# Output buffers, split distance and build steps of a decoder block's last projection tiles

## The chip, the cores and the metric

The kernel runs on one core of a Trainium2 chip. A core has a matrix engine (TensorE, PE in the profile; PEld is its weight load), a vector engine (VectorE, DVE), an activation engine (ScalarE, ACT), GpSimd (POOL) and SyncE (SP), which here only starts transfers between the chip's main memory (DRAM) and the on-chip memory (SBUF). Matrix products land in accumulators (PSUM). Every engine works through its own list of instructions in the order in which they stand, and waits at an instruction until what that instruction needs has happened; instructions on different engines are tied by semaphores alone. The metric is the device time of one run in microseconds (us); lower is better.

## The reference

One decoder layer on a sequence of 2048 positions and 1024 channels, in float32. A normalised input `h` is projected to eight blocks of 1024 columns; one half feeds a recurrent branch, the other an attention branch; each branch is multiplied by its gate and projected back, the two are merged with gates computed from `h`, and one more projection with a residual and a last normalisation gives the output:

```
y_rnn  = (hr * silu(z_rnn)) @ w_out_rnn
y_attn = (o * silu(z_attn)) @ w_out_attn
merged = sigmoid(g_r + bg_r) * y_rnn + sigmoid(g_a + bg_a) * y_attn
x      = x + gate * (merged @ w_o)
out    = rms_norm(x, g_final)
```

The changed code computes the third line's sum for part of `y_attn`, tile by tile, and at the same time prepares `w_o` for the fourth.

## The kernel before, in words

**Products in three parts.** float32 products are made from operands that are split into a high part (`hi_act`, line 158, on ACT) and a low rest (`lo_pool`, line 164, on POOL, or `lo_dve`, line 167, on DVE). `mm3` multiplies high by high, high by low and low by high: three matmuls of 128x512 per 128 rows of the inner dimension, all recorded at line 150.

**The projection generator.** `steps` works through 64 tiles of 128 output rows by 512 positions: eight jobs of eight tiles, the first four for `w_out_rnn`, the last four for `w_out_attn`. A tile is eight steps (`k` from 0 to 7), and a step is one `mm3`, so a tile has 24 matmuls. Weights come in half tiles numbered `x = 2 * t + k // 4`. The first 40 tiles (`TAIL0`) are spread between the units of the attention as filler. The last 24, tiles 40 to 63, run behind it without other matmuls, 192 steps in all, step `s` being `k` of tile `40 + s // 8`. Jobs change at steps 0, 64 and 128. This stretch is called the tail here.

**What one tail tile needs.** Two half tiles of weights of 256 KB are loaded on SP (line 1675) into a ring of six buffers (`S0` to `S3`, `st3`, `st4`), five half tiles ahead, and split by `split_w`: the high part on ACT, the low part on DVE for even half tiles and on POOL for odd ones. Two gate tiles of 256 KB (`gaT`, the sigmoid gate, and `mrT`, the recurrent branch's share) are loaded on SP by `load_g` (line 1715). When the tile's matmuls are done, `evict` multiplies the accumulator by the gate (line 1720) and adds the share (line 1722) on DVE, in place in the gate's buffer; `store` (line 1727) sends that buffer to `meT` on SP. There are two accumulators `pj`. `evict` of tile `t - 1` stands at `k == 1` of tile `t`, its `store` at `k == 4`, the gate load of tile `t + 1` at `k == 3`. Gates have four buffers named `fg`; every third tile takes `s1` and `s2` in their place.

**Operands of the next job.** The eight right operands of a job (`yh`, `yl`) are loaded and split at steps that stand in `LATE_LOAD_Y` and `LATE_SPLIT_Y`, where step 8 is the first step of the new job. Operands 5 and 6 land in `st1`, 7 in `st2`, the other five in the ring `R`.

**Building the last projection's operands.** The last projection (`merged @ w_o`) is made with fewer products from sums of blocks of `w_o`. `build_rows(s, k)` prepares row blocks `k` of these operands, for `k` from 0 to 3, over 21 steps: two rows loads of 512 KB into `st1` and `st2` (`load_rows`, line 1859; on SP for `k` 0, on ACT's queue for the others), two products with the broadcast gate on POOL (line 1862), four sums on DVE (line 1870) and seven splits. They start at steps 8, 33, 78 and 142. All of this is written out by hand: `fire(s)` issues what `on` has noted for step `s`, inside `tc.manual_schedule()`, so the order in the code is each engine's order. After step 192 the last projection begins (tiles `X`, `Z`, `W`, `V`, `Y`).

The core of the order within a tail tile:

```python
if k % KH == 2 and x >= 2 * TAIL0:
    for x1 in (x + 2, x + 3) if x == 2 * TAIL0 + 1 else (x + 2,) if x == 2 * TAIL0 else (x + 3,):
        split_w(x1)
if k == 1 and t:
    evict(t - 1, last)
...
    if k == 4:
        store(t - 1)
    for x in g_loads.pop((t - TAIL0, k), ()):
        load_g(TAIL0 + x)
```

Of the kernel before, what the change touches and what calls it, by code (L numbers as in the profile page):

```python
# [10 lines left out]
F32 = mybir.dt.float32  # L11
# [4 lines left out]
ALU = mybir.AluOpType  # L16
# [4 lines left out]
P = 128  # L21
S = 2048
D = 1024
KT = D // P
NB = 4
CH = 512
# [63 lines left out]
def decoder_block(ctx, tc, x, c, positions, g_norm, w_mod, b_mod, w_in, b_gate, conv_w, conv_b,  # L90
                  w_a, b_a, w_x, b_x, lam, w_out_rnn, w_out_attn, w_o, g_final, cst, out):
    nc = tc.nc
    cnt = [0]

    def T(pool, shape, dt, tag, **kw):
        cnt[0] += 1
        return pool.tile(shape, dt, tag=tag, name=f"{tag}_{cnt[0]}", **kw)
# [17 lines left out]
    gateD = scratch("gateD", [1, D])  # L115
# [565 lines left out]
    with tc.manual_schedule():  # L681
# [45 lines left out]
        for j in range(4):  # L727
# [15 lines left out]
            if j == 1:  # L743
                raws[1, 2] = load_wv_raw(1, 2)
                raws[1, 4] = load_wv_raw(1, 4)
                x1 = load_x(hp, 1, "T", 14)
# [362 lines left out]
    for t in range(6):  # L1109
        pieces = []  # L1110
        i0 = t * P
        while i0 < (t + 1) * P:
            hd, i = divmod(i0, 96)
# [155 lines left out]
    for f in range(2):  # L1269
        if f:  # L1270
            pools.close("xp")
            vx = pools.open("vx", bufs=1)
            x1 = load_x(hp, 3, "T", 14)
# [55 lines left out]
    fl = pools.open("fl", side="right", bufs=1)  # L1329
# [27 lines left out]
    class Head:  # L1357
# [255 lines left out]
        def load_gate(self):  # L1613
            self.y = {}
            self.zt = T(ap_, [P, 2, 4, P], F32, "zt", bufs=2)
            cols = slice(self.bk[0] * CH, (self.bk[1] + 1) * CH)
            nc.sync.dma_start(self.zt[:].rearrange("p i r j -> p i (r j)"),
                              zaT[self.h * P : (self.h + 1) * P, cols].rearrange("p (i q) -> p i q", i=2))
# [35 lines left out]
    TAIL0 = KT * (NB + 1)  # L1654
# [3 lines left out]
    def steps(jobs):  # L1658

        tiles = [(j, m) for j in range(len(jobs)) for m in range(KT)]  # L1660
        Y, G = {}, {}
# [15 lines left out]
        def split_w(x):  # L1677
            if RAW < x < 2 * len(tiles):
                raw = W[x][:, 1].bitcast(F32)
                hi_act(W[x][:, 0], raw)  # L1680
                (lo_pool if x % 2 else lo_dve)(W[x][:, 1], raw, W[x][:, 0])
# [23 lines left out]
        def load_g(t):  # L1705
            j, m = tiles[t]
            w, ys, n = jobs[j]
            at_ = slice(m * P, (m + 1) * P), slice(n * CH, (n + 1) * CH)
            G[t] = []
            for src in (grT,) if ys is yaT else (gaT, mrT):  # L1710
                if t >= TAIL0 and (t - TAIL0) % 3 == 2 and t < TAIL0 + 21:
                    g = T(fp, [P, CH], F32, ("s1", "s2")[len(G[t])])
                else:
                    g = T(fl, [P, CH], F32, "fg", bufs=4)
                nc.sync.dma_start(g[:], src[at_])
                G[t].append(g)

        def evict(t, ps):
            g = G[t]
            nc.vector.tensor_tensor(g[0][:], ps[:], g[0][:], ALU.mult)  # L1720
            if len(g) > 1:
                nc.vector.tensor_tensor(g[0][:], g[0][:], g[1][:], ALU.add)

        def store(t):
            j, m = tiles[t]
            w, ys, n = jobs[j]
            nc.sync.dma_start((mrT if ys is yaT else meT)[m * P : (m + 1) * P, n * CH : (n + 1) * CH], G.pop(t)[0][:])

        g_loads = {(0, 0): [0], (23, 0): [23]}
        for x in range(22):  # L1730
            g_loads[x, 3] = [x + 1]
        for k in range(KT):
            split_y(0, k)
        yield
# [1 line left out]
        for t, (j, m) in enumerate(tiles):  # L1736
            ps = T(pj, [P, CH], F32, "pj")
            for k in range(KT):
                x = 2 * t + k // KH
                if k % KH == 1:  # L1740

                    if x < 2 * TAIL0:
                        load_w(x + 3)
                    for x1 in range(x + 3 if x == 2 * TAIL0 else x + 5, x + 6) if x >= 2 * TAIL0 else ():
                        load_w(x1)
                if k % KH == 2 and x >= 2 * TAIL0:
                    for x1 in (x + 2, x + 3) if x == 2 * TAIL0 + 1 else (x + 2,) if x == 2 * TAIL0 else (x + 3,):
                        split_w(x1)
                if k == 1 and t:
                    evict(t - 1, last)  # L1750
                if t < TAIL0:
                    if k == 3:
                        load_g(t)
                    if k == 7 and t:
                        store(t - 1)
                else:
                    if k == 4:
                        store(t - 1)
                    for x in g_loads.pop((t - TAIL0, k), ()):
                        load_g(TAIL0 + x)  # L1760
                wt = W[2 * t + k // KH]
                yh, yl = Y[j, k]
                mm3(ps[:], wt[:, 0, k % KH, :], wt[:, 1, k % KH, :], yh[:], yl[:], first=k == 0, last=k == KT - 1)
                if k % KH == KH - 1:
                    W.pop(2 * t + k // KH)


                x = m * KT + k - KT * (KT - 1)
                j1 = j + 1
                if m == 0:  # L1770
                    x, j1 = x + KT * KT, j

                for k1 in (LATE_LOAD_Y if t >= TAIL0 else LOAD_Y).get(x, ()) if j1 else ():
                    load_y(j1, k1, t)
                for k1 in (LATE_SPLIT_Y if t >= TAIL0 else SPLIT_Y).get(x, ()) if j1 else ():
                    split_y(j1, k1)
                yield
            last = ps
# [13 lines left out]

    LOAD_Y = {-12: [0], -10: [1], -8: [2], -6: [3], -2: [4], 4: [5], 5: [6], 6: [7]}
    SPLIT_Y = {-3: [0], 3: [1], 4: [2], 5: [3], 7: [4], 10: [5], 11: [6], 12: [7]}
    LATE_LOAD_Y = {-12: [0], -10: [1], -8: [2], -6: [3], -2: [4], -1: [5, 6, 7]}
    LATE_SPLIT_Y = {-3: [0], 1: [1], 2: [2], 3: [3], 6: [4], 8: [5], 9: [6], 10: [7]}
    fill = steps([(0, yaT, n) for n in range(NB)] + [(1, oT, n) for n in range(NB)])
    next(fill)
    with tc.manual_schedule():
# [42 lines left out]
    def stage(i, shape, dt=F32):  # L1842
        return T(fp, shape, dt, f"st{i}")
# [3 lines left out]
    def on(n, fn, *args):  # L1847
        pend.setdefault(n, []).append((fn, args))
# [5 lines left out]
    v = {}  # L1854
# [204 lines left out]

    LAST = 3 * KT * KT  # L2060
    with tc.manual_schedule():
        v["gate"] = stage(0, [P, D])
        nc.sync.dma_start(v["gate"][:], gateD[0:1, :].broadcast_to([P, D]))
        for k, x in enumerate((8, 33, 78, 142)):
            build_rows(x, k)
            for i in range(2):
                on(max(x - 7 + 3 * i, 2 * i), load_rows, k, i)
        on(LAST - 20, load_left, 0)
        for p in range(NP):
            for d, fn, args in left_events(p):  # L2070
                x = 7 * p + d - 4
                if p or d > 2:
                    on_p(max(x, 1), fn, *args)
                else:
                    on(LAST - 10 + 3 * (d + 1), fn, *args)
            if p:
                on_p(max(7 * p - 12, 0), load_left, p)
            if p > 1:
                on_p(7 * p - 2, load_rows_x, p)
        for s in range(LAST):  # L2080
            next(fill)
            fire(s)
        next(fill, None)
        fire(LAST)
        assert not pend
        pools.close("fl", "pR")
        up.append(pools.open("up", side="right", bufs=1))
        fire_p()
        load_rows_x(0)
        load_rows_x(1)  # L2090
        v["gf"] = T(up[0], [P, D], F32, "gf")
        nc.sync.dma_start(v["gf"][:], g_final.unsqueeze(0).broadcast_to([P, D]))
        for p in range(NP):
            output_pair(p)
        assert not after
# [30 lines left out]
```

## Time and profile before

| | us |
|---|---|
| median of 3 runs | 2245.62 |
| lowest and highest | 2242.92 to 2248.07 |
| profiled execution, its own time | 2247.45 |
| span of the profile | 2245.7 |
| TensorE busy in the span | 2177.2 |
| VectorE busy | 1446.2 |
| ScalarE busy | 1289.7 |
| GpSimd busy | 1087.1 |

Times in the trace count from the start of the span. A matmul's recorded length is longer than its share of the pipeline: matmuls that follow each other start 0.227 us apart while one is recorded with 0.39 us, so distances between starts are what tells the pace. The tail runs from about 1917 us to 2084 us, the last projection from there to the end. In a timeline row, the bracket names how long the engine stood idle before the instruction and what ended it. A row of transfers on SP or ACT has the time that the issue took, not the time of the transfer.

### The profile page before, as it was taken

To read this page: it belongs to the slowest core of one execution; us is meant where nothing else is said; L and a number is where in the kernel's file an instruction comes from. 1 tells how busy PE (TensorE), PEld (TensorE's weight loads), DVE (VectorE), ACT (ScalarE), POOL (GpSimd) and SP (SyncE) were. 2 spreads that over 40 slices of the span, in tenths; PEclk is the share of its full clock that TensorE was granted. 3 is DMA by queue.
4 is the path that set the end of the run, shared out by engine and by line. 5 is a ranking of instruction groups with operands and counts; after the bars stand their busy time and mean duration, and the time that the engine had idled before them with its cause. 6 is when DMAs were issued, how large, how long until landed. Compare 5 with 4: busy or idle time off the path is not lost.

```text
span 2245.7 us, 34220 instructions
## 1 busy us (share of the span) xinstructions
PE 2177.2 (97%) x11326; PEld 1837.3 (82%) x11326; DVE 1446.2 (64%) x2475; ACT 1289.7 (57%) x2570; POOL 1087.1 (48%) x807
## 2 busy tenths in 40 slices
PE   8999999999999999999999999999999999889998
PEld 4998888888777998888888877888988988667886
DVE  5838887878455815444445442666777776586787
ACT  5637678667533627556546202777888886233333
POOL 2457777767556422223222102556666564465443
PEclk9999999999999999999999999999999999999999
DMA  8367887887998378888999988878887787788543
GB/s 276 115 218 258 282 295 269 292 284 266 332 280 278 113 233 271 280 290 289 299 302 299 360 290 279 266 229 255 270 258 237 229 260 226 246 249 279 185 162 113
DMA packets 412277, 573.41 MB, mean 255 GB/s; under 512 B 72422, under 2 KB 270274, under 8 KB 411076
## 3 DMA queue, kind: packets, MB, share of 16 engines
q1 hardware_dynamic: 369892, 442.82, 63.0%
q10 hardware_dynamic: 42016, 128.36, 14.9%
q8 instruction: 90, 1.47, 0.3%
q14 instruction: 87, 0.71, 0.1%
q0 software_dynamic: 192, 0.05, 0.0%
HBM read 352.99 MB, written 218.11 MB: 254 GB/s over the span
## 4 chain that ended last, share of the span: by engine, by line
PE 50%; DMA 8%; issue 4%; DVE 4%; POOL 3%; ACT 2%; SPq 2%; ACTq 0%; POOLq 0%; DVEq 0%
PE X L150 10%; PE V L150 9%; PE pj L150 7%; PE W L150 5%; PE Z L150 5%; PE Y L150 4%; PE sc L150 3%; PE o L150 3%; DMA R<-in_w_in_dram 1%; PE pg L150 1%; PE pT L1505 1%; DMA kraw<-kT 1%; PE pT L1518 1%; DMA S<-wR 1%; DMA kraw<-qT 1%
## 5 line engine op out<-in xcount | busy, mean ns | idle before, releaser
L150 PE MATMUL pj<-yh,S 128*128 128x512 f32 x896 | 330.8, 410 | 12.7 <-DVE fg L1720 7.2
L164 POOL TENSOR_TENSOR S<-R,S 128x512 fp32r<-128x512 f32 x168 | 251.9, 1507 | 175.8 <-ACT S L158 73.8
L150 PE MATMUL X<-T,S 128*128 128x512 f32 x1344 | 324.3, 390 | 4.3 <-POOL S L164 4.2
L150 PE MATMUL V<-T,S 128*128 128x512 f32 x1344 | 324.6, 390 | 3.7 <-DVE t L454 3.4
L150 PEld LDWEIGHTS V<-T,S 128*128 128x128 f32 x1344 | 251.8, 188 | 58.4 <-ACT S L158 2.6
L150 PEld LDWEIGHTS X<-T,S 128*128 128x128 f32 x1344 | 251.4, 188 | 58.7 <-POOL S L164 5.1
L150 PEld LDWEIGHTS pj<-yh,S 128*128 128x128 f32 x896 | 172.1, 192 | 46.5 <-issue 9.2
L164 POOL TENSOR_TENSOR S<-s,S 128x512 fp32r<-128x512 f32 x92 | 139.7, 1518 | 114.7 <-ACT S L158 66.8
L150 PE MATMUL pj<-yl,S 128*128 128x512 f32 x448 | 179.7, 401 | 4.5 <-POOL yl L164 2.8
L1421 ACT ACTIVATE pp<-pp,st 128x256 f32<-128x256 f32 (+3 forms) x256 | 133.7, 525 | 59.7 <-DVE st L1420 59.2
L150 PE MATMUL Z<-T,S 128*128 128x512 f32 x672 | 162.0, 390 | 0.0
L150 PE MATMUL Y<-T,S 128*128 128x512 f32 x672 | 161.8, 390 | 0.0
L150 PE MATMUL W<-T,S 128*128 128x512 f32 x672 | 161.7, 389 | 0.0
L150 PEld LDWEIGHTS W<-T,S 128*128 128x128 f32 x672 | 126.0, 188 | 27.0 <-issue 0.9
L167 DVE TENSOR_TENSOR ptl<-pT,pth 128x384 fp32r<-128x384 f32 (+1 forms) x160 | 97.9, 629 | 77.3 <-ACT pth L158 75.1
L150 PEld LDWEIGHTS Y<-T,S 128*128 128x128 f32 x672 | 125.9, 188 | 26.0
L150 PEld LDWEIGHTS Z<-T,S 128*128 128x128 f32 x672 | 125.8, 188 | 26.1
L164 POOL TENSOR_TENSOR s<-R,s 128x512 fp32r<-128x512 f32 x32 | 46.1, 1439 | 205.3 <-ACT s L158 150.1
L912 DVE SCALAR_TENSOR_TENSOR xc<-xr,par,xc 128x512 f32<-128x512 f32 x96 | 99.4, 1036 | 46.4 <-ACT xc L906 44.1
L158 ACT ACTIVATE S<-R 128x512 fp32r<-128x512 f32 x168 | 101.8, 623 | 46.2 <-DMA R<-in_w_in_dram 18.2
L1485 ACT ACTIVATE pp<-pp,M 128x256 f32<-128x256 f32 (+3 forms) x256 | 118.3, 526 | 9.7 <-DVE M L1608 9.7
L1420 DVE CUSTOM_DVE_ANT_0 pp<-sc,msk 128x256 f32<-128x256 f32 (+3 forms) x256 | 103.6, 448 | 28.5 <-PE sc L150 27.6
(405 smaller groups left out, 4999.1 us busy)
## 6 DMA issues: line engine op xcount, KB each, us to landing
sD<-S ACTq DMA_DIRECT2D x196, 512.0 KB, 4.4
S<-sD SPq DMA_DIRECT2D x196, 512.0 KB, 5.2
S<-wD SPq DMA_DIRECT2D x82, 512.0 KB, 5.3
R<-in_w_in_dram SPq DMA_DIRECT2D x136, 256.0 KB, 4.4
wD<-s ACTq DMA_DIRECT2D x64, 256.0 KB, 5.5
T<-in_w_mod_dram SPq DMA_DIRECT2D x8, 1024.0 KB, 11.7
vN<-ev SPq DMA_DIRECT2D x64, 128.0 KB, 2.8
zaT<-ev SPq DMA_DIRECT2D x32, 256.0 KB, 4.6
```

What stands on the lines that cost most here:

```text
L150: nc.tensor.matmul(o, lhsT=l, rhs=r, start=st, stop=sp, **kw)
L158: nc.scalar.activation(o, i, AF.Copy)
L164: nc.gpsimd.tensor_tensor(o, i, h.bitcast(F32), ALU.subtract)
L167: return nc.vector.tensor_tensor(o, i, h.bitcast(F32), ALU.subtract).ins
L912: nc.vector.scalar_tensor_tensor(xc, xr[:, i : i + CH], cw(i), xc, ALU.mult, ALU.add)
L1420: nc.vector.tensor_tensor_reduce(pdst, s_ps, mask, 1.0, 3e38, ALU.add, ALU.min, m_)
L1421: nc.scalar.activation(pdst, pdst, AF.Exp, bias=m_, scale=-1.0, accum_out=l_)
L1485: nc.scalar.activation(pp, pp, AF.Copy, scale=w)
L1505: nc.tensor.transpose(pt[:, c0 + j * P : c0 + (j + 1) * P], pp[i][:, k * P : (k + 1) * P], ident)
L1518: nc.tensor.transpose(pt[:, c * P : (c + 1) * P], pp[:, half * P : (half + 1) * P], ident)
```

## The change

- `load_g` always takes the four `fg` buffers. `evict` writes its result to `s1` or `s2` in turn for tiles 40 to 61 (`o`), and `store` sends that buffer; tiles 62 and 63 stay in place.
- The gate load of tile `t + 1` still stands at `k == 3`, the first at `k == 0` of tile 40; the `store` moves from `k == 4` to `k == 6`.
- `split_w` is called for half tile `x + 2` in place of `x + 3`.
- Operand 7 of a late job is loaded four steps later and split one step later.
- The broadcast gate is loaded at step 5 in place of ahead of step 0. The builds start at steps 14, 75, 100 and 142, and their row loads move with them.
- The first left operands of the last projection are prepared one step later (`LAST - 9` in place of `LAST - 10`).

```diff
             for src in (grT,) if ys is yaT else (gaT, mrT):
-                if t >= TAIL0 and (t - TAIL0) % 3 == 2 and t < TAIL0 + 21:
-                    g = T(fp, [P, CH], F32, ("s1", "s2")[len(G[t])])
-                else:
-                    g = T(fl, [P, CH], F32, "fg", bufs=4)
+                g = T(fl, [P, CH], F32, "fg", bufs=4)
                 nc.sync.dma_start(g[:], src[at_])
                 G[t].append(g)
 
         def evict(t, ps):
             g = G[t]
-            nc.vector.tensor_tensor(g[0][:], ps[:], g[0][:], ALU.mult)
+            o = T(fp, [P, CH], F32, f"s{1 + t % 2}") if TAIL0 <= t < TAIL0 + 22 else g[0]
+            nc.vector.tensor_tensor(o[:], ps[:], g[0][:], ALU.mult)
             if len(g) > 1:
-                nc.vector.tensor_tensor(g[0][:], g[0][:], g[1][:], ALU.add)
+                nc.vector.tensor_tensor(o[:], o[:], g[1][:], ALU.add)
+            g[0] = o
...
-        g_loads = {(0, 0): [0], (23, 0): [23]}
-        for x in range(22):
-            g_loads[x, 3] = [x + 1]
...
                 if k % KH == 2 and x >= 2 * TAIL0:
-                    for x1 in (x + 2, x + 3) if x == 2 * TAIL0 + 1 else (x + 2,) if x == 2 * TAIL0 else (x + 3,):
-                        split_w(x1)
+                    split_w(x + 2)
...
-                    if k == 4:
+                    if k == 0 and t == TAIL0:
+                        load_g(t)
+                    if k == 3 and t + 1 < len(tiles):
+                        load_g(t + 1)
+                    if k == 6:
                         store(t - 1)
-                    for x in g_loads.pop((t - TAIL0, k), ()):
-                        load_g(TAIL0 + x)
...
-    LATE_LOAD_Y = {-12: [0], -10: [1], -8: [2], -6: [3], -2: [4], -1: [5, 6, 7]}
-    LATE_SPLIT_Y = {-3: [0], 1: [1], 2: [2], 3: [3], 6: [4], 8: [5], 9: [6], 10: [7]}
+    LATE_LOAD_Y = {-12: [0], -10: [1], -8: [2], -6: [3], -2: [4], -1: [5, 6], 3: [7]}
+    LATE_SPLIT_Y = {-3: [0], 1: [1], 2: [2], 3: [3], 6: [4], 8: [5], 9: [6], 11: [7]}
...
-        v["gate"] = stage(0, [P, D])
-        nc.sync.dma_start(v["gate"][:], gateD[0:1, :].broadcast_to([P, D]))
-        for k, x in enumerate((8, 33, 78, 142)):
+        def load_gate():
+            v["gate"] = stage(0, [P, D])
+            nc.sync.dma_start(v["gate"][:], gateD[0:1, :].broadcast_to([P, D]))
+
+        on(5, load_gate)
+        for k, x in enumerate((14, 75, 100, 142)):
             build_rows(x, k)
             for i in range(2):
-                on(max(x - 7 + 3 * i, 2 * i), load_rows, k, i)
+                on(x - 7 + 3 * i, load_rows, k, i)
...
-                    on(LAST - 10 + 3 * (d + 1), fn, *args)
+                    on(LAST - 9 + 3 * (d + 1), fn, *args)
```

## The prediction

> **What bounds the kernel now.** I read the chain of waits for the pace of TensorE, then the windows, one stage to a row, then the timelines of the stages that lose time, and SP's waits. In the windows each engine has its busy time and, after x, its instructions; then come the granted clock, the share of the DMA engines and GB/s.
>
> ```profile
> 2086.55 2.72 PE Z L150 x12
> ...
> core 0: us, PE busy (x) PEld busy (x) DVE busy (x) ACT busy (x) POOL busy (x), PEclk, DMA share, GB/s
> 1916.90:1932.80 15.90, 13.67 (x47) 9.20 (x46) 7.38 (x8) 4.20 (x7) 4.28 (x3) 0.89 0.75 270
> 1932.80:1945.60 12.80, 5.64 (x26) 4.36 (x24) 5.26 (x5) 2.30 (x4) 7.69 (x5) 0.92 0.80 236
> 1945.60:1967.10 21.50, 19.39 (x73) 14.95 (x73) 17.84 (x18) 8.21 (x15) 13.29 (x8) 0.89 0.77 244
> 1967.10:1992.90 25.80, 20.46 (x73) 15.85 (x74) 23.65 (x22) 11.06 (x20) 17.19 (x12) 0.80 0.79 234
> 1992.90:2025.65 32.75, 32.75 (x146) 26.93 (x144) 24.30 (x25) 9.96 (x17) 17.83 (x11) 1.00 0.85 257
> 2025.65:2041.50 15.85, 13.25 (x49) 9.65 (x48) 9.38 (x10) 7.78 (x13) 8.91 (x6) 0.89 0.93 312
> 2041.50:2057.80 16.30, 16.30 (x73) 13.52 (x72) 9.83 (x10) 4.74 (x8) 9.53 (x6) 1.00 0.88 276
> 2057.80:2083.70 25.90, 23.70 (x98) 19.10 (x97) 20.06 (x23) 6.60 (x11) 9.37 (x6) 0.93 0.71 230
> 2083.70:2245.70 162.00, 152.44 (x673) 125.91 (x671) 132.78 (x225) 56.89 (x115) 71.04 (x48) 0.98 0.44 155
> ```
>
> Twelve matmuls at pace take 2.72 us, so a tile of 24 takes 5.44. The eight windows of the tail hold 2, 1, 3, 3, 6, 2, 3 and 4 tiles; what each has over 5.44 a tile is lost: 5.0, 7.4, 5.2, 9.5, 0.1, 5.0, 0 and 4.1, together 36.3 us of 166.8. The ninth window, the last projection, is TensorE at work and isn't touched. So the most that the change can win is some 36 us. The fifth and seventh windows show that the tail can run at pace, also while builds are under way.
>
> ```profile
> 1945.59 0.77 PE L150 MATMUL pj<-yh,S 128*128 128x512 f32 x1 [7.16 <-DVE fg L1720]
> ...
> 1967.08 0.47 PE L150 MATMUL pj<-yh,S 128*128 128x512 f32 x1 [1.48 <-ACT S L158]
> ...
> 1982.93 0.77 PE L150 MATMUL pj<-yh,st 128*128 128x512 f32 x1 [4.71 <-DVE fg L1720]
> ...
> 2065.63 0.47 PE L150 MATMUL pj<-yh,S 128*128 128x512 f32 x1 [2.20 <-ACT T1h L158]
> ```
>
> The two longest gaps end with `evict` (line 1720): TensorE waited for an accumulator. After the second, the fourth window's granted clock is 0.80: of its 9.5 us, 4.7 and a few tenths are gaps, about 4.5 slower matmuls. Why is `evict` late?
>
> ```profile
> SPq L1715 <- DMA meT<-fg: 32.5, 12, 4.8
> SPq L1727 <- DVE fg L1722: 23.2, 8, 7.9
> SPq L1715 <- DVE fg L1722: 18.5, 4, 6.4
> ```
> ```profile
> 1934.04 0.32 SPq L1715 DMA_DIRECT2D fg<-mrT  x1
> ...
> 1935.41 0.92 SPq L1675 DMA_DIRECT2D S<-wR  x2
> ```
> ```profile
> 1930.83 0.68 DVE L1720 TENSOR_TENSOR fg<-pj,fg 128x512 f32<-128x512 f32 x1
> ...
> 1941.52 1.66 DVE L167 TENSOR_TENSOR S<-S 128x512 fp32r<-128x512 f32 x1 [7.51 <-ACT S L158]
> 1943.10 1.75 DVE L167 TENSOR_TENSOR B11l<-st,B11h 128x512 fp32r<-128x512 f32 x1
> 1944.77 0.68 DVE L1720 TENSOR_TENSOR fg<-pj,fg 128x512 f32<-128x512 f32 x1
> ```
>
> SP's waits in the tail (total us, times, longest) say that SP stands 12 times, 32.5 us in all, at a gate load into a buffer whose result, stored in place, has not left yet. The weights queue behind it. In the second window the load waits for `evict` at 1930.83 and its store, goes out at 1934.04, the weights at 1935.41; their split on DVE stands idle for 7.51 us until 1941.52, and the next `evict`, queued behind it and a build's split, comes at 1944.77. So the loop is `evict`, store, gate, weights, split, `evict`; it runs over three tiles, 16.3 us at pace, and this turn took 13.9 without slack anywhere.
>
> **The change, part by part.** *Separate result buffers, store at `k == 6`.* From tile 43 on a gate load no longer waits for a store, only for the `evict` two steps ahead of it. SP loses the 32.5 us wait. The loop shrinks by the store:
>
> ```profile
> L1720 DVE TENSOR_TENSOR fg<-pj,fg x20: 676/680/692, 1903.3 to 2086.4; 128x512 f32<-128x512 f32 x20
> L1722 DVE TENSOR_TENSOR fg<-fg,fg x20: 693/1066/2647, 1904.1 to 2087.1; 128x512 f32<-128x512 f32 x20
> ...
> DMA to landing us min/median/max: 2.4/4.9/8.0
> ```
> ```profile
> S<-wR SPq DMA_DIRECT2D x30, 256.0 KB, 5.9
> ```
>
> These rows give durations in ns (min/median/max), the landing time of the transfers with the gate buffers, and 5.9 us for a weight load. The loop becomes `evict` 1.7, weights 5.9, high part about 0.7, split 0.7 to 1.7: 9 to 10 us, estimated, against 16.3. The new wait: `evict` of `t + 1` overwrites the buffer stored 11 steps earlier, 7.5 us at pace. The median store (4.9) fits, the longest (8.0) misses by 0.5, below what a tile can absorb: nothing. Two instructions and two transfers a tile stay as they are. Behind a waiting store on SP stand weight loads that are needed more than 8 us later.
>
> The first two gate loads of the tail behind tile 40 still need the old stores, but the order has `evict` of tile 40 ahead of the split that waits on weights. The load now at 1934.04 can go out near 1926.9 when DVE does that `evict` at its slot, the weights some 8 us earlier; issued at 1927.4 they land at 1933.3, are split by 1935.3, ahead of 1938.3, where tile 43 begins if tile 42 runs 5.44 from 1932.83. The 7.16 goes; I leave 1 us for tiles 42 to 44. The third window's 5.2 is mainly the slow matmuls after that gap, clock 0.89, and goes with it; a build's residue (1 us) stays.
>
> *Splits two half tiles ahead in place of three.* The same 48 pairs of splits, later by four steps. A load has 13 steps, 8.8 us, to its split (9 before, 6.1, against the 5.9 above), so splits stop waiting. The price: a split precedes its use by 6 steps, 4.1 us, and not by 10; with its own duration DVE may be late by 3.1 us without TensorE noticing. Before, the accumulator set that bound at 7 steps less `evict`'s 0.7, 4.1.
>
> *Builds at 14, 75, 100 and 142 for 8, 33, 78 and 142.* Work is the same: 8 DVE operations and 2 long POOL products each.
>
> ```profile
> 1970.25 0.68 DVE L1870 TENSOR_TENSOR st<-st 128x512 f32<-128x512 f32 x1
> ...
> 1982.11 0.68 DVE L1720 TENSOR_TENSOR fg<-pj,fg 128x512 f32<-128x512 f32 x1
> ...
> 2013.83 0.68 DVE L1720 TENSOR_TENSOR s<-pj,s 128x512 f32<-128x512 f32 x1
> ...
> 2019.13 0.68 DVE L1720 TENSOR_TENSOR fg<-pj,fg 128x512 f32<-128x512 f32 x1
> ```
>
> The build of step 33 put `evict` of tile 46 at 1982.11. Its slot is the second step of tile 47, 5.44 + 0.68 behind tile 46's start at 1967.08: 8.9 us late, the 4.71 gap. The build of step 78 put those of tiles 51 and 52 at 2013.83 and 2019.13, some 4.0 and 3.8 behind slots reckoned likewise from 1992.88, and TensorE lost nothing. With the job change at step 64 between, the first build had the gate wait and new operands beside it; the second had neither. I take the second: the builds alone at 14 and 142 cost 1 each, and the change at 64, now free of a build, 1. The two at 75 and 100 stand 25 steps apart and lag into each other: 4.0 and 4.0 less 3.1 are 4.9, and 0.6 for a clock that falls after a short stop: 5.5. Ends: nothing, and the 9.5 of the fourth window.
>
> *Operand 7 four steps later, and the change at 128.* The second build of the pair ends at step 121, and operands 5 and 6 go into `st1` from 119: SP may stand there as it did before, 3.4 us:
>
> ```profile
> SPq L1693 <- DVE T4l L167: 3.4, 1, 3.4
> ```
>
> The sixth window loses 5.0 at this change, also with stores in its chain:
>
> ```profile
> 2020.56 6.53 DMA meT<-fg
> 2027.11 5.64 DMA fg<-mrT
> 2032.76 4.62 DMA fg<-gaT
> ```
>
> A store of 6.53 leaves the chain, the loads stay: I take 3, with ends 0 and 5. *Gate broadcast at step 5, left operands a step later:* one 512 KB load leaves the queue ahead of step 0, and nothing waits for it before step 14's products; the last operand is then ready three matmuls later at the latest, 0.7 us, which I hide behind tile 63. Its cost without cover is 0.7.
>
> *Start.* Tiles 40 and 41 lose 5.0 to operands and weights issued ahead of all this; I keep 5.1 with rounding.
>
> The sum of what remains: 5.1 start, 1 at tiles 42 to 44, 1 first build, 1 change at 64, 5.5 pair, 3 change at 128, 1 last build: 17.6. From 36.3 this is a gain of 18.7. The profiled execution took 2247.45, 1.8 above the median: 2228.8 against it, 2227 against the median. Within the parts' ends the forecast runs from 2220 to 2233.
>
> **Rivals.** *R1, DVE and POOL shut each other out.* The addition from two SBUF inputs took 693 to 2647 ns, the product with one input in PSUM 676 to 692. If a DVE operation on two SBUF inputs and a POOL operation never overlap, a build needs 8 of 0.68 (the first row of the block above) plus two products and three splits on POOL:
>
> ```profile
> 1996.49 2.39 POOL L1862 TENSOR_TENSOR st<-st,st 128x1024 f32<-128x1024 f32 x1 [3.08 <-DMA st<-in_w_o_dram]
> 2000.41 1.29 POOL L164 TENSOR_TENSOR st<-st 128x512 fp32r<-128x512 f32 x1 [1.53 <-ACT st L158]
> ```
>
> That is 5.4 + 4.8 + 3.9 = 14.1 of exclusive time, and a tile adds 2 of 0.68 and 1.29, 2.65. The pair's 46 steps are 31.3 us and 5.75 tiles: 28.2 + 15.2 = 43.4, 12.1 too many. Less 3.1 of slack, plus 4.5 for the clock: 13.5 for 5.5, so 2235. For it: those stretched rows; against it: the fifth window lost 0.1 with one build in it.
>
> The Trainium skill states this exclusion ("SBUF — State Buffer", section "Who interferes with whom"): a DVE instruction with two SBUF inputs and a GpSimd one that reads SBUF hold a shared pair of ports for a whole instruction each, while one SBUF input does not contend. The two rows of line 1720 and line 1722 agree. By it the pair is the change's weak place, and the sum would be R1's, 2235 and not 2227.
>
> *R2, slower: splits with less lead.* If each of the four builds puts DVE 8.9 us behind as the one of step 33 did, TensorE now stands 8.9 − 3.1 = 5.8 and loses 4.5 of clock, 10.3 a build. Four make 41.2 in place of 7.5, and with the other 10.1 the loss is 51.3, 15 over before: 2261. It decides from 6.6 us a build on, 26.2 in all. For it: the lead is truly shorter, and in the fourth window DVE was at work almost throughout, 23.65 of 25.80, so this lag was its own work and not late weights. Against: that work held a job change as well, and the build of 78 had less than half the lag.
>
> *R3, transfers are the bound.* The windows' GB/s times their lengths make 42.4 MB for the tail. At the fifth window's 257 GB/s that takes 165 us of the 166.8: a gain of 2, 2244. Against it: 312 and 276 GB/s in other windows; the forecast's tail of 148 us needs 286, within them but not by much.
>
> **How the numbers follow.** Forecast 0.55, R1 0.18, R2 0.17, R3 0.10. 0.2%, 4.5 us, is about what a measurement of this kernel can tell from no change; R3 falls into it, with little of the others. Faster 0.73, same 0.10, slower 0.17. The range reaches from 2216, the forecast's 2220 with a start that gains 4 too, to 2244 with R3; R2 is left out.
>
> **What would show it.** Right: SP's wait at line 1715 for `meT` near zero; no gap of several us at tiles 42 and 43; gaps ended by a split (line 167 or 158) instead of line 1720, most of them at steps 75 to 125; the tail some 148 us long with the clock above 0.95. Wrong: `evict` lags beyond 6 us in the builds at 14 and 142 (R2); DVE rows of 1.8 us filling steps 75 to 125 (R1); weight loads landing 8 us and more behind their issue at an unbroken DMA share of 0.9 (R3).

## The result, and the profile after

The changed kernel takes 2239.92 us (median of 16 runs, 2232.50 to 2242.48) against 2244.99 for the kernel before (16 runs): ratio 0.9974, 95% interval 0.9964 to 0.9984. It is faster by 5 us by the medians and 5.8 by the ratio. The forecast was 2227, a gain of 18.7, so the sign was right, the range held the time, and more than two thirds of the gain did not come.

The profiled execution took 2237.5 us, 2.4 below its median, where that of before lay 2.5 above its own. Some of the 10 us between the two profiles is thus scatter: the projection's matmuls run alone from 1910.3 us on in the one and from 1908.6 in the other (over all runs below, 1904.5 to 1911.2). Profiles are used here to see where time goes, medians and intervals to see whether it goes.

The windows of the changed kernel, cut where tiles 40, 42, 45, 48, 51, 54, 57, 60 and 63 begin:

```profile
core 0: us, PE busy (x) PEld busy (x) DVE busy (x) ACT busy (x) POOL busy (x), PEclk, DMA share, GB/s
1914.80:1930.20 15.40, 13.53 (x50) 9.71 (x49) 6.83 (x8) 4.21 (x8) 4.64 (x4) 0.89 0.86 278
1930.20:1950.50 20.30, 18.23 (x74) 14.60 (x73) 14.39 (x15) 7.43 (x14) 11.66 (x7) 0.92 0.87 281
1950.50:1968.30 17.80, 16.57 (x73) 13.43 (x72) 11.80 (x14) 5.61 (x10) 9.08 (x7) 1.00 0.90 281
1968.30:1988.45 20.15, 17.76 (x73) 13.20 (x72) 11.11 (x12) 6.40 (x11) 10.85 (x7) 1.00 0.93 312
1988.45:2013.00 24.55, 19.75 (x74) 14.18 (x73) 19.73 (x20) 9.06 (x16) 16.31 (x11) 0.93 0.75 233
2013.00:2035.20 22.20, 18.58 (x74) 14.32 (x73) 21.39 (x20) 10.37 (x20) 16.73 (x10) 0.92 0.83 266
2035.20:2051.50 16.30, 16.30 (x73) 13.51 (x72) 15.53 (x14) 5.71 (x10) 10.66 (x6) 1.00 0.93 281
2051.50:2068.30 16.80, 16.63 (x73) 13.43 (x72) 13.56 (x14) 4.73 (x8) 8.48 (x6) 1.00 0.83 285
2068.30:2073.75 5.45, 5.45 (x26) 4.50 (x24) 3.24 (x5) 0.63 (x1) 0.00 (x0) 1.00 0.16 61
```

Against 10.88 us for two tiles and 16.32 for three, the losses are 4.5, 4.0, 1.5, 3.8, 8.2, 5.9, 0, 0.5 and 0: 28.4 us, where the forecast left 17.6. The tail takes 159.0 us, where the forecast had 148. The kernel before lost 36.7, counted from tile 40's first matmul at 1916.47; the prediction's first window opens 0.4 us behind it, so its 36.3 and its 5.0 for the start are each 0.4 too low. Nearly all of the 10.8 us between forecast and trace is in tiles 42 to 56: tiles 48 to 56 hold 17.9 of the 28.4, where the forecast had 9.5 for the pair of builds and the two job changes.

Four of TensorE's longer gaps behind the start in the changed kernel, with what ended them (the longest of all, at 2027.64, stands with the second build below):

```profile
1941.03 0.74 PE L150 MATMUL pj<-yh,S 128*128 128x512 f32 x2 [2.07 <-POOL S L164]
...
1952.34 0.73 PE L150 MATMUL pj<-yh,st 128*128 128x512 f32 x2 [1.23 <-DVE st L167]
...
1999.75 0.50 PE L150 MATMUL pj<-yh,S 128*128 128x512 f32 x1 [1.20 <-ACT S L158]
...
2006.25 0.84 PE L150 MATMUL pj<-yh,S 128*128 128x512 f32 x2 [1.61 <-DVE S L167]
```

No gap in the tail ends with `evict` any more; each ends with a split of weights or of an operand. SP's waits in the changed kernel (line 1712 is the gate load, 1718 and 1720 the two operations of `evict`):

```profile
SPq L1712 <- DVE s L1718: 37.3, 17, 5.0
...
SPq L1712 <- DVE s L1720: 10.7, 17, 2.1
...
SPq L1712 <- DMA meT<-fg: 1.1, 1, 1.1
...
SPq L1712 <- DMA meT<-s: 0.7, 1, 0.7
```

The wait of gate loads for stores is gone, as said; in its place SP waits 48 us in all for `evict`, which the gate load of the next tile but one now follows directly.

### The profile page after: what moved, and what is told of

The parts are those of the page before. It is cut to its first block, busy times and chain, and to the rows that moved or that the text cites. A ratio compares the mean times of both kernels' runs of the same rounds, so it can differ in the third digit from the quotient of the medians.

```text
span 2235.7 us, 34221 instructions
## 1 busy us (share of the span) xinstructions
PE 2173.8 (97%) x11326; PEld 1833.5 (82%) x11326; DVE 1448.3 (65%) x2475; ACT 1288.2 (58%) x2570; POOL 1093.0 (49%) x807
## 4 chain that ended last, share of the span: by engine, by line
PE 49%; DMA 8%; issue 4%; DVE 3%; POOL 3%; ACT 2%; SPq 2%; ACTq 0%; POOLq 0%; DVEq 0%
PE X L150 10%; PE V L150 9%; PE pj L150 7%; PE W L150 5%; PE Z L150 5%; PE Y L150 4%; PE sc L150 3%; PE o L150 3%; PE pg L150 1%; DMA R<-in_w_in_dram 1%; DMA meT<-s 1%; PE pT L1505 1%; DMA kraw<-qT 1%; PE pT L1518 1%; DMA S<-wD 1%
## 5 line engine op out<-in xcount | busy, mean ns | idle before, releaser
L150 PE MATMUL pj<-yh,S 128*128 128x512 f32 x896 | 331.5, 411 | 11.9 <-DVE S L167 5.2
L164 POOL TENSOR_TENSOR S<-R,S 128x512 fp32r<-128x512 f32 x168 | 256.8, 1536 | 170.1 <-ACT S L158 67.7
L150 PE MATMUL Z<-T,S 128*128 128x512 f32 x672 | 162.0, 390 | 0.0
```

The costliest lines, as they stand in the source:

```text
L150: nc.tensor.matmul(o, lhsT=l, rhs=r, start=st, stop=sp, **kw)
L164: nc.gpsimd.tensor_tensor(o, i, h.bitcast(F32), ALU.subtract)
```

## The experiments

The table gives the time, the ratio to the kernel before, and the loss in us per three tiles of that run's profile (tile 42 to 44, 45 to 47, and so on), worked out from the starts of the tiles' first matmuls. Each run has its own measurement of the kernel before beside it (medians 2242.16 to 2243.67 for the runs from only_out on), so rows are compared by their ratios.

The losses come from one profile of each kernel. How far they scatter is seen in tiles 42 to 47, up to which the changed kernel, noload, noprod, build1gone and build2gone have the same instructions in the same order: they lose 3.0 to 4.0 there and then 1.5 to 3.6. A difference of 2 us between two such numbers says nothing by itself.

| run | median us | ratio (95%) | 42 | 45 | 48 | 51 | 54 | 57 | 60 |
|---|---|---|---|---|---|---|---|---|---|
| before | 2244.99 | 1 | 10.2 | 7.3 | 4.5 | 0.1 | 5.0 | 0 | 4.1 |
| changed | 2239.92 | 0.9974 (0.9964 to 0.9984) | 4.0 | 1.5 | 3.8 | 8.2 | 5.9 | 0 | 0.5 |
| only_out | 2238.88 | 0.9979 (0.9970 to 0.9989) | 7.3 | 7.7 | 4.4 | 0.4 | 4.4 | 0 | 1.2 |
| only_split | 2232.71 | 0.9953 (0.9939 to 0.9966) | 7.4 | 3.2 | 3.5 | 1.1 | 1.9 | 0 | 1.6 |
| split3 | 2242.61 | 0.9997 (0.9988 to 1.0005) | 7.7 | 1.5 | 3.5 | 2.9 | 11.1 | 0 | 1.7 |
| oldbuild | 2234.71 | 0.9967 (0.9955 to 0.9980) | 6.7 | 2.1 | 2.7 | 1.8 | 3.9 | 0 | 1.9 |
| spload | 2238.28 | 0.9981 (0.9969 to 0.9992) | 2.9 | 2.0 | 4.4 | 6.8 | 7.8 | 0 | 1.1 |
| noload | 2232.82 | 0.9956 (0.9940 to 0.9971) | 3.4 | 3.6 | 1.0 | 0.7 | 7.6 | 0 | 0.9 |
| noprod | 2233.92 | 0.9958 (0.9943 to 0.9972) | 3.1 | 3.6 | 1.2 | 3.2 | 5.6 | 0 | 0.9 |
| build1gone | 2230.98 | 0.9947 (0.9935 to 0.9959) | 3.0 | 3.6 | 1.4 | 0 | 6.5 | 0 | 0.5 |
| build2gone | 2233.60 | 0.9959 (0.9947 to 0.9970) | 4.0 | 1.7 | 4.4 | 4.3 | 1.0 | 0.2 | 2.6 |
| store4 | 2236.73 | 0.9968 (0.9955 to 0.9981) | 2.4 | 2.0 | 1.8 | 5.5 | 7.2 | 0 | 1.2 |
| alldve | 2233.11 | 0.9956 (0.9940 to 0.9973) | 5.3 | 0 | 2.9 | 2.2 | 8.0 | 0 | 0 |
| before_alldve | 2229.46 | 0.9945 (0.9932 to 0.9958) | 6.7 | 3.4 | 4.1 | 0.1 | 2.5 | 2.1 | 0 |
| ob_alldve | 2228.99 | 0.9937 (0.9921 to 0.9953) | 6.9 | 0.8 | 2.7 | 0.5 | 3.5 | 0.9 | 0 |
| best2 | 2225.92 | 0.9931 (0.9914 to 0.9948) | 5.3 | 1.1 | 3.4 | 0 | 1.2 | 0 | 0 |
| best3 | 2230.03 | 0.9949 (0.9936 to 0.9962) | 6.7 | 0.2 | 4.0 | 0 | 4.2 | 0 | 0 |

### Which part brings the gain

**only_out**: the kernel before with the result buffers, the gate loads and the store at the seventh step, and nothing else. Its diff against the changed kernel, in part:

```diff
-                    split_w(x + 2)
+                    for x1 in (x + 2, x + 3) if x == 2 * TAIL0 + 1 else (x + 2,) if x == 2 * TAIL0 else (x + 3,):
+                        split_w(x1)
...
-        for k, x in enumerate((14, 75, 100, 142)):
...
+        for k, x in enumerate((8, 33, 78, 142)):
...
```

> The kernel before with one part of the change: results into s1 and s2, gates always in fg, store at the seventh step. Splits three half tiles ahead, builds at 8, 33, 78, 142 and the operand loads as before. If the in-place store was what made weights late (my forecast), the 7.16 us gap at tile 43 goes and the tail loses some 20 to 25 us in place of 36: ratio about 0.994. If the builds are what costs, by instructions queued in order on ACT, POOL and DVE, the tail loses 28 or more: ratio 0.997 or above.

**split3**: the changed kernel with the first three lines of that diff, and its builds where the change put them.

> The changed kernel with the splits three half tiles ahead again. If the shorter lead of the splits is what ate the forecast gain (every gap after the change ends with a split), this is faster than the changed kernel by 5 to 10 us: ratio to before 0.993 to 0.995. If the splits are late because ACT, POOL and DVE stand in order behind a build's row loads, the gaps move to the accumulator and the time stays within 3 us of the changed kernel: 0.996 to 0.999.

**only_split**: the kernel before with `split_w(x + 2)` and nothing else.

> The kernel before with one part of the change: weights split two half tiles ahead in place of three. If late weight loads behind the in-place store hold DVE and with it evict, four steps more for each load take 2.7 us from each such wait: 8 to 12 us less, ratio 0.995 to 0.997. If the store's chain sets the pace alone, 0.999 to 1.001, the gaps ending with splits in place of evict.

The result buffers alone bring 0.21%, in the second of the two ranges that I gave, the one against my forecast; the shorter split distance alone brings 0.47%, in the first range given for it and nearly twice the whole change (the intervals, 0.9939 to 0.9966 and 0.9964 to 0.9984, just overlap). Taken back from the changed kernel, it takes the gain along (0.9997). Of the two cases that I gave for split3, a longer lead that helps and no difference, neither came: it is slower. The waits for weights in the tail (total us, times, longest) show how. First before:

```profile
ACT S L158 <- DMA S<-wR: 33.3, 10, 10.6
ACT st L158 <- DMA st<-wR: 16.9, 5, 7.0
...
PE pj L150 <- DVE fg L1720: 12.2, 3, 7.2
```

With the result buffers alone (only_out):

```profile
ACT S L158 <- DMA S<-wR: 34.1, 15, 7.7
ACT st L158 <- DMA st<-wR: 17.1, 7, 6.9
PE pj L150 <- DVE s L1718: 10.3, 4, 5.0
```

The gap at the start of tile 43, 7.16 us before, is shorter there and still ends with `evict`:

```profile
1936.38 0.77 PE L150 MATMUL pj<-yh,S 128*128 128x512 f32 x1 [4.37 <-DVE s L1718]
```

With the split distance alone (only_split):

```profile
ACT S L158 <- DMA S<-wR: 20.8, 7, 6.4
ACT st L158 <- DMA st<-wR: 10.4, 4, 3.5
...
SPq L1715 <- DMA meT<-fg: 27.2, 11, 4.6
SPq L1715 <- DMA meT<-s: 12.1, 5, 3.8
```

ACT waited 50.2 us for weights before and 51.2 with the result buffers: they took SP's wait for stores away and set SP's wait for `evict` in its place, and TensorE still waited 10.3 us for `evict`. With splits four steps later ACT waits 31.2 us, although SP stands at stores for 39.3 us (44.4 before), and no row of TensorE waiting for `evict` is left. So moving the split is enough: what held `evict` was the split that stood ahead of it in DVE's order and waited for the load. What earlier loads alone would bring isn't shown, for in only_out ACT waits for them as long as before.

### What moving the builds did

**oldbuild**: the changed kernel with the old build steps and the gate broadcast at the start.

```diff
...
-        on(5, load_gate)
-        for k, x in enumerate((14, 75, 100, 142)):
+        v["gate"] = stage(0, [P, D])
+        nc.sync.dma_start(v["gate"][:], gateD[0:1, :].broadcast_to([P, D]))
+        for k, x in enumerate((8, 33, 78, 142)):
...
-                on(x - 7 + 3 * i, load_rows, k, i)
+                on(max(x - 7 + 3 * i, 2 * i), load_rows, k, i)
```

> The changed kernel with the builds at 8, 33, 78 and 142 again and the gate broadcast ahead of step 0. If moving the builds clear of the job changes helps as the forecast said, this is slower than the changed kernel by 5 us or more: ratio 1.000 and above. If the pair costs the same wherever it stands, because the second build's row loads wait for the first build, it is within 3 us: 0.996 to 0.999; the loss then sits in steps 26 to 54 in place of 93 to 121.

Its ratio is 0.9967 against 0.9974, with intervals that overlap over most of their length: moving the builds gained nothing that these runs can tell. Tiles 42 to 50 lose 11.5 with old steps, for 9.3, and tiles 51 to 56 far less (5.7 for 14.1). The time is what the second case of my expectation had; its reason, the same loss in another place, isn't borne out by the profile, in which tiles 51 to 56 are the dearer place.

**spload**: row loads of all builds on SP.

```diff
-        (nc.scalar if k else nc.sync).dma_start(t[:], w_o[0, (k + i * KH) * P : (k + i * KH + 1) * P, :])
+        nc.sync.dma_start(t[:], w_o[0, (k + i * KH) * P : (k + i * KH + 1) * P, :])
```

> The changed kernel with the row loads of all builds issued on SP, where before those of builds 1 to 3 stood on ACT's queue. If ACT standing at these issues (until the first build of the pair has read st1 and st2) makes the high parts of weights late, the gaps of 1.2 and 0.4 us ended by ACT and some of the 1.8 us one go, 3 to 6 us, ratio 0.994 to 0.996. If the pair's cost is DVE and POOL shutting each other out, it stays at 0.997 with the same gaps, ended by DVE and POOL. If SP standing there makes the weights late instead, 0.998 and above.

No difference from the changed kernel that these runs can tell (0.9981 lies in the range of the third case, but the intervals overlap), and tiles 51 to 56 lose 14.6 as against 14.1: the queue on which the loads stand is not what matters. The profile suggests why: ACT's first high part waits for the rows anyway.

**noload** and **noprod**: the pair without its row loads, and without its products. The diff is that of noload, in part; the row loads of these two builds are left out besides. noprod leaves out the product's line for the same builds.

```diff
     def gate_rows(k, i):
-        nc.gpsimd.tensor_tensor(v[k, i][:], v[k, i][:], v["gate"][:], ALU.mult)
+        if k in (1, 2):
+            v[k, i] = stage(1 + i, [P, D])
+        nc.gpsimd.tensor_tensor(v[k, i][:], (v["gate"] if k in (1, 2) else v[k, i])[:], v["gate"][:], ALU.mult)
```

> The changed kernel; the row loads of builds 1 and 2 (steps 75 and 100) are left out and their products made from the gate tile itself, so the result is not the layer's; POOL, DVE and ACT have the same instructions. If the pair's loss is row loads that land late and hold POOL's product, ACT's first high part and the weight splits queued behind it, tiles 51 to 56 lose some 5 us in place of 14: ratio 0.993 to 0.994. If it is DVE and POOL shutting each other out (R1), they still lose 12 or more: 0.997.

> The changed kernel; the two POOL products of builds 1 and 2 are left out and the rows used as loaded, so the result is not the layer's; the row loads stay. 9.6 us less work on POOL that reads SBUF. If DVE and POOL shut each other out, tiles 51 to 56 lose 9 us less, ratio 0.993; if late row loads hold ACT, they gain only the product's own 2.4 us a time, about 4 us, ratio 0.995 to 0.996.

**build1gone** and **build2gone**: one build of the pair left out (the diff is that of build1gone, in part).

```diff
-        for k, x in enumerate((14, 75, 100, 142)):
+        for k, x in ((0, 14), (2, 100), (3, 142)):
```

> The changed kernel without the build at step 75, likewise (the last projection uses the operands of the build at 14 twice). If the second build lags because the first holds its row loads and its engines, tiles 48 to 50 lose 1 in place of 3.8, tiles 51 to 53 some 2 in place of 8.2, and tiles 54 to 56 about 4 in place of 5.9: ratio 0.992 to 0.994. If each build costs by itself, tiles 51 to 53 stay at 5 or more.

> The changed kernel without the build at step 100 (its operands are not made, the last projection uses those of the build at 142 twice, so the result is not the layer's). If the loss of tiles 54 to 56 is that build's work beside the operand splits of the change at 128, they lose 2 us in place of 5.9, and tiles 51 to 53 some 2 to 3 in place of 8.2: tail 9 to 10 us shorter, ratio 0.993. If the job change alone makes it, tiles 54 to 56 stay at 5 to 6.

Without the row loads, tiles 48 to 53 lose 1.7 us instead of 12.0, although all instructions of POOL, DVE and ACT are there; without the products, 4.4. Tiles 54 to 56 kept their loss in both, and the times came less far down than I wrote of noload (0.9956 for 0.993 to 0.994), with an interval that overlaps the changed kernel's; noprod's 0.9958 is what I wrote of late rows. Without the first build of the pair the time is 0.9947, for 0.992 to 0.994, and without the second 0.9959, for 0.993. The window of tiles 51 to 53 in noload, then that of tiles 51 to 53 in build1gone:

```profile
1988.30:2005.30 17.00, 16.57 (x73) 13.42 (x72) 16.83 (x17) 7.45 (x13) 12.30 (x8) 1.00 0.78 226
```
```profile
1989.60:2005.90 16.30, 16.30 (x73) 13.50 (x72) 8.18 (x11) 4.72 (x8) 9.93 (x6) 1.00 0.89 292
```

How the loads act is seen in the changed kernel's rows of ACT and POOL:

```profile
1974.77 0.63 ACT L158 ACTIVATE yh<-st 128x512 fp32r<-128x512 f32 x1 [1.89 <-DMA st<-oT]
1974.87 0.35 ACTq L1856 DMA_DIRECT2D st<-in_w_o_dram  x1
...
1976.15 0.36 ACTq L1856 DMA_DIRECT2D st<-in_w_o_dram  x1
...
1984.79 0.63 ACT L158 ACTIVATE B11h<-st 128x512 fp32r<-128x512 f32 x1 [7.07 <-POOL st L1859]
...
2002.79 0.33 ACTq L1856 DMA_DIRECT2D st<-in_w_o_dram  x1
2003.22 1.15 ACT L158 ACTIVATE S<-S 128x512 fp32r<-128x512 f32 x2 [2.48 <-POOL T1l L164]
```
```profile
1982.35 2.40 POOL L1859 TENSOR_TENSOR st<-st,st 128x1024 f32<-128x1024 f32 x1 [5.02 <-DMA st<-in_w_o_dram]
1984.71 1.29 POOL L164 TENSOR_TENSOR S<-S 128x512 fp32r<-128x512 f32 x1
```

The first build of the pair gets its rows late. Both loads stand behind operand 7 of the job at step 64, which the change itself loads four steps later and which lands just ahead of 1974.77: the first in ACT's order behind that operand's high part, the second until its split has read `st2`. The rows land some 7 us later (7.3 in the median of the two); POOL stands 5.02 us at the product, ACT 7.07 us at the first high part, and weight splits stand behind both. The second build's row loads then stand on ACT until the first build's last split on POOL has read `st2` (2002.79), and hold the high parts at 2003.22. Leaving out the first build removes both, and tiles 51 to 53 lose nothing; leaving out the second removes the hold, with that build's first operations, and they lose 4.3.

A rival is a late store. In the changed kernel DVE stands at an `evict` in tile 50 for a store that was issued just behind the row loads, and noload has no such wait, perhaps because it moves less:

```profile
1984.82 0.69 DVE L1718 TENSOR_TENSOR s<-pj,fg 128x512 f32<-128x512 f32 x1 [5.87 <-DMA meT<-s]
```

In build1gone DVE stands twice like that within tiles 52 and 53, for 3.69 and 4.15 us, and they still lose nothing:

```profile
2001.66 0.69 DVE L1718 TENSOR_TENSOR s<-pj,fg 128x512 f32<-128x512 f32 x1 [4.15 <-DMA meT<-s]
```

So a wait of 4 us for a store costs nothing by itself there. How much the longer one adds beside late rows is open, and so is what the rows would cost with operand 7 loaded at its old step.

Tiles 54 to 56 are another matter: noload leaves them at 7.6, build1gone at 6.5, and build2gone brings them to 1.0. There DVE does the second build's last operations and the operand splits of the change at 128 together. Its rows in the changed kernel:

```profile
2022.42 1.78 DVE L167 TENSOR_TENSOR yl<-R,yh 128x512 fp32r<-128x512 f32 x1
2024.13 1.77 DVE L167 TENSOR_TENSOR T4l<-st,T4h 128x512 fp32r<-128x512 f32 x1
2025.83 1.75 DVE L167 TENSOR_TENSOR S<-S 128x512 fp32r<-128x512 f32 x1
2027.51 1.76 DVE L167 TENSOR_TENSOR yl<-R,yh 128x512 fp32r<-128x512 f32 x1
```
```profile
2027.64 1.22 PE L150 MATMUL pj<-yh,S 128*128 128x512 f32 x2 [2.61 <-DVE S L167]
```

The split at 2025.83 stands behind them and ends at 2027.58; TensorE, whose matmul needs it, goes on at 2027.64, 2.8 us later than at pace. So the builds are not clear of the job change at 128: the one at step 100 runs into it.

### Stretched DVE rows, and late stores

**alldve**: low parts of the tail's weights and of the builds on DVE only. **before_alldve** does this alone to the kernel before.

```diff
-                (lo_pool if x % 2 else lo_dve)(W[x][:, 1], raw, W[x][:, 0])
+                (lo_pool if x % 2 and x < 2 * TAIL0 else lo_dve)(W[x][:, 1], raw, W[x][:, 0])
...
-            (14, high, "B21", k), (14, low, "B22", k, lo_pool), (15, low, "B21", k, lo_dve), (15, high, "T3", k),
-            (16, high, "T2", k), (17, low, "T3", k, lo_pool), (17, combine, "T4", k, "B21", "T2", sub),
+            (14, high, "B21", k), (14, low, "B22", k, lo_dve), (15, low, "B21", k, lo_dve), (15, high, "T3", k),
+            (16, high, "T2", k), (17, low, "T3", k, lo_dve), (17, combine, "T4", k, "B21", "T2", sub),
...
-            (19, high, "T4", k), (20, high, "T1", k), (21, low, "T4", k, lo_dve), (21, low, "T1", k, lo_pool)):
+            (19, high, "T4", k), (20, high, "T1", k), (21, low, "T4", k, lo_dve), (21, low, "T1", k, lo_dve)):
```

> The changed kernel with all low parts of the tail's weights and of the builds on DVE, so that POOL has only the products and half the operand splits. By R1's bookkeeping the exclusive time of a build falls from 14.1 to 12.3 and that of a tile from 2.65 to 2.05: 7 us less for the pair, ratio 0.994 to 0.995. If order and late rows are the cause, DVE has more queued in order ahead of evict and nothing is gained: 0.997 to 1.000.

> The kernel before with nothing changed but all low parts of the tail's weights and builds on DVE. If the stretched DVE rows are what made evict late before, the gap of 4.71 us with its slow clock goes, ratio 0.996; if the chain of store, gate load and weight load sets the pace, DVE's longer queue behind each late weight adds to it: 0.999 to 1.003.

Two groups of DVE from tile 42 on (busy us, mean ns), of the changed kernel and of alldve:

```profile
L1867 DVE TENSOR_TENSOR st<-st,st 128x512 f32<-128x512 f32 x12 | 13.6, 1133 | 2.4 <-POOL st L1859 2.3
L167 DVE TENSOR_TENSOR st<-st 128x512 fp32r<-128x512 f32 x7 | 11.4, 1629 | 0.0
```
```profile
L167 DVE TENSOR_TENSOR st<-st 128x512 fp32r<-128x512 f32 x14 | 9.5, 683 | 0.0
L1867 DVE TENSOR_TENSOR st<-st,st 128x512 f32<-128x512 f32 x12 | 8.2, 683 | 0.0
```

Twice the splits take less of DVE's time when POOL makes none of them. The Trainium skill's page "SBUF — State Buffer", section "Who interferes with whom", says that a DVE instruction with two SBUF inputs and a GpSimd instruction that reads SBUF exclude each other for a whole instruction; these rows, 1629 ns and 683 ns, agree. The kernel before gains 0.55% by it, more than by the change itself. The changed kernel gains 0.18%, with intervals that overlap; its 0.9956 lies between the two cases that I gave. But the exclusion alone isn't the pair's price, as R1 had it: in noload's window above, 17 DVE instructions still take 16.83 us, 0.99 each as in the changed kernel's (20 in 19.73), and tiles 48 to 53 lose 1.7. With shorter splits these tiles lose 5.1 of their 12.0, with stretched splits and no rows to wait for 1.7: most of the loss needs both. In tiles 54 to 56 alldve gains nothing (8.0).

**store4**: the store at the fifth step again.

```diff
-                    if k == 6:
+                    if k == 4:
                         store(t - 1)
```

> The changed kernel with the store at the fifth step of a tile again, 1.36 us earlier. Three evicts of the changed kernel's trace waited for the landing of the store two tiles back, 0.3, 0.6 and 2 us behind their slots. If that wait costs TensorE time, these go and the time falls by up to 2 us, ratio 0.9965; if the splits set the end, no difference from the changed kernel: 0.997 to 0.998.

Inconclusive: its interval and that of the changed kernel overlap over most of their length, and single runs lie at 2231 to 2233 and at 2236 to 2243. The wait itself is real; this group of the changed kernel's `evict` names its idle time:

```profile
L1718 DVE TENSOR_TENSOR s<-pj,fg 128x512 f32<-128x512 f32 x21 | 14.4, 685 | 18.3 <-DMA meT<-s 12.6 <-PE pj L150 5.6
```

### A faster version

**ob_alldve**: the changed kernel with both the diffs of oldbuild and alldve. **best2**: besides, the store at `k == 4` and the row loads of the two later builds three steps earlier. **best3**: as best2, with results in place as before the change.

```diff
-                on(max(x - 7 + 3 * i, 2 * i), load_rows, k, i)
+                on((max(x - 7 + 3 * i, 2 * i), x - 7 + 3 * i, x - 10 + 3 * i, x - 10 + 3 * i)[k], load_rows, k, i)
```

> The changed kernel with the builds at 8, 33, 78, 142 and all low parts of the tail's weights and builds on DVE. If moving the builds cost (row loads between a job's operand buffers and the first build) and the exclusion of DVE and POOL cost separately, the two gains add up: some 3 to 5 us below either alone, ratio 0.993 to 0.995. If they are the same microseconds, it stays at 0.9955 to 0.967 of these two runs, that is 0.9955 to 0.997.

(The 0.967 there is a slip of the pen for 0.9967.)

> The same with the store at the fifth step and the row loads of the two later builds three steps earlier. If late row loads and late stores still delay the splits there, 1 to 3 us below the run with old build steps and low parts on DVE: 0.992 to 0.994. If what is left is the start and the two job changes, the same as that run.

> The fastest run so far (old build steps, low parts on DVE, row loads of the later builds three steps earlier) without the separate result buffers: results in place, s1 and s2 for every third tile's gates, as before. If the separate buffers add nothing beside splits two half tiles ahead, 0.992 to 0.995 as with them; if they take a wait that the splits' four steps don't cover, slower by 3 us or more: 0.9955 or above.

Old steps and DVE's low parts together give 0.9937, at least the sum of the two gains. best2 is the fastest, 2225.92 us, 0.9931 (0.9914 to 0.9948): by the ratios some 15 us below the kernel before and 10 below the changed one. Against best3 (0.9949, 0.9936 to 0.9962) it isn't separated: whether the result buffers add anything beside the other parts stays open. best2 and ob_alldve aren't separated either, and neither is best2 from before_alldve (0.9945, 0.9932 to 0.9958), the kernel before with nothing but its low parts moved to DVE.

## Why the prediction was right and wrong

**What held.** The tail alone changed: the last projection takes 162.0 us in both. SP's wait for stores went from 44.4 us (32.5 and 11.9) to under 2; gaps of TensorE now end with splits; the gap of 7.16 us at the start of tile 43 is gone, the longest in tiles 42 to 44 being 2.07; the last three stages lose next to nothing, and the transfers weren't the bound (R3): the window of tiles 57 to 59 ran at pace with 281 GB/s, and the tail shortened further in runs that move the same bytes (best2). R2 showed its sign once: tile 43 starts at 1935.63, so the slot of its `evict` in the build at 14 is 1941.75, and it starts at 1949.19, 7.4 us later. In the build at 142 no `evict` is more than 2.4 us late. No `evict` holds TensorE, R2's 10.3 us for each build did not come (tiles 42 to 47 lose 5.5), and with the lead given back, in split3, the kernel is slower.

**The step that failed: the price of the builds and the job changes beside them.** "I take the second: the builds alone at 14 and 142 cost 1 each, and the change at 64, now free of a build, 1", and 5.5 for the pair, 3 for the change at 128. Measured: 4.0 and 1.5 where the first build stands, 3.8, 8.2 and 5.9 for the change at 64, the pair and the change at 128: 23.4 for 11.5, with the 1 for tiles 42 to 44 among the 11.5. I costed the instructions of a build and the lag between two builds on DVE. I didn't follow the row loads, which the step moves along: behind a job change they cannot go out until the operands have left `st1` and `st2`, and with 25 steps between the builds those of the second wait for the first. With these loads left out (noload), 10.3 of the 12.0 us of tiles 48 to 53 are gone. I had noted the conflict at step 119, on SP, and overlooked the one at 68 and 93, on ACT. The pair's work beside the change at 128 was seen as a wait of SP for `st1`; it is DVE's queue, with that build's work in it: without the build, tiles 54 to 56 lose 1.0 in place of 5.9 (build2gone).

**R1** gave 2235, 5 us below the measured time, as R3's 2244 is 4 above it. Its 13.5 us for the pair, with 1 and 3 for the two changes, make 17.5 where tiles 48 to 56 lose 17.9. That agreement is luck: noload keeps the exclusion and loses 9.3 there, and next to nothing in tiles 48 to 53. What R1 named is there, though, and worth more than I gave it: taking it away gains 0.18% by the ratios in the changed kernel (their intervals overlap) and 0.55% in the one before.

**The shares of the parts.** "Separate result buffers" got most of the forecast gain. "Splits two half tiles ahead in place of three" got the remark that splits stop waiting, no share of the gain, and a price of 1 us of slack. The runs turn that round: 0.21% and 0.47% alone, and the gain of both together with old builds, 0.33%, is no more than that of the splits. I had named the gate load's new wait for `evict` and put it at nothing in the loop of 9 to 10 us: SP is still held (57.5 us in only_out), and the gap that I had going altogether, 7.16, is still 4.37 with the buffers alone. The 4 steps of lead that the splits lose, 2.7 us, mattered less than the 4 steps that DVE no longer stands waiting.

**The first build.** With the loads at steps 7 and 10, the rows land late there too: tiles 42 to 47 lose 5.5 for 2. That the row loads did it here too is argued from this row of the changed kernel's POOL alone; no run changed these loads without their build:

```profile
1934.54 4.76 POOL L1859 TENSOR_TENSOR st<-st,st 128x1024 f32<-128x1024 f32 x2 [5.11 <-DMA st<-in_w_o_dram]
```

## What to carry to other kernels

When a load may come late, put the instruction that waits for it late in its engine's order, as near to its use as the slack allows: alone, that brought more here than taking one of the waits from the queue that issues the loads, since what hurts is the work queued behind the waiting instruction. When a block of work is moved, follow its loads first: into which buffers, who read them last, and which engine's order the issue stands in. And try each part of a change alone: here one line of it was worth nearly twice the whole.

## What was not expected

Stores from the result buffers took 5.8 us in the median of the changed kernel, by its transfers, and one of them 8.47 by its chain of waits:

```profile
meT<-s SPq DMA_DIRECT2D x22, 256.0 KB, 5.8
```
```profile
1976.22 8.47 DMA meT<-s
```

The 7.5 us of distance that I had reckoned with didn't cover the longest, and DVE stood 12.6 us at `evict` for stores. And moving work from POOL to DVE, the busier engine, made DVE's own groups shorter: 14 splits in 9.5 us in place of 7 in 11.4.
